# Which experts of the first sparse tile are added on TensorE: every third of the first 72 instead of the last 43

## The chip, the cores and the metric

One Trainium2 chip, of which the program uses one core. The metric is the time of one execution on the device in microseconds, as a median over runs. The core's engines are TensorE (PE, with its weight loads shown apart as PEld), VectorE (DVE), ScalarE (ACT), GpSimd (POOL) and SyncE (SP); each runs its own instructions in the order in which they stand in its queue and waits for the others by semaphores. Matrix products are accumulated in eight PSUM banks of 128 x 512 float32.

## What is computed

One decoder layer in float32 on 512 tokens of width 1024: an RMSNorm and one input projection; sparse attention (8 heads; compressed, selected and window branches) beside a diagonal state-space group; an output projection; then a product-key expert layer, and a last RMSNorm. The experts are where the change lies:

```python
s1 = einsum('bchd,kd->bchk', q[..., :half], sub1)
s2 = einsum('bchd,kd->bchk', q[..., half:], sub2)
v1, i1 = top_k(s1, 16); v2, i2 = top_k(s2, 16)
cand = v1[..., :, None] + v2[..., None, :]
cidx = i1[..., :, None] * 128 + i2[..., None, :]
top, sel = top_k(cand, 16)            # 16 of 16384 experts, for each of 8 heads
eidx = take_along_axis(cidx, sel); gate = softmax(top)
u_sel = u_tab[eidx]; v_sel = v_tab[eidx]
hid = einsum('bcd,bchkd->bchk', xb, u_sel)
act = gelu(hid) * gate
out = einsum('bchk,bchkd->bcd', act, v_sel)
```

So every token has 128 experts: a dot with a row of u, a gelu with a gate, and a row of v, times that number, added to the token.

## The kernel before

The tokens are four tiles of 128. Tiles 0 and 1 are sparse: for each k from 0 to 127 one indirect DMA, issued by POOL, gathers the k-th expert's u and v rows of all 128 tokens (128 x 2048 floats, 1.05 MB). Tiles 2 and 3 are dense: `dense` (l. 1215 to 1348) goes over all 16384 experts with matmuls, and its loop takes most of the second half of the program. Tile 1's experts all run inside that loop (class `Steps`, l. 1129), its adds on DVE.

Tile 0's experts run ahead of the loop, beside the generator `rest()` (l. 1461 to 1529): the projections of tiles 1 to 3 (keys, compressed keys and values, queries), `compress`, the attention of tile 1, the gated linear unit, the mix and the route of tile 1, beside it the attention and mix of tiles 2 and 3, and the route of tiles 2 and 3. A route ends in many small sorting steps on DVE (top 16 of 128, twice, then of the candidates). Each step of `rest()` yields a credit (table `W`, l. 1458), and the loop at l. 1544 to 1549 runs as many experts as the credit allows.

Expert k in the generator `peer` (l. 1070 to 1127): the gather is issued `ahead` = 2 experts early into a slot of a ring of five; DVE makes the dot into `hid` (l. 1098); ACT makes `act` in five steps (l. 1103 to 1107); and `lag` = 2 experts later the v row is added, in one of two ways that the lambda `HOW` (l. 1537) chooses:

- "V": DVE adds v times act to the token's row h (l. 1120).
- "P": ACT writes a diagonal matrix `dg` of act (l. 1115, three buffers), and PE adds dg times v to two PSUM banks `acc`, in two halves of 512 columns (l. 1117). The banks are taken at the first such expert (l. 1113) and held until `flush` (l. 1078) adds them to h after expert 127.

Behind the add the slot goes back to the ring (l. 1121), and the gather of expert k + 5 may use it. Ahead of the dense loop, all engines' orders are made by the framework's scheduler from program order, dependencies and its own timing of them (l. 1647); once written, each engine's queue is fixed. In the dense loop the order is pinned by hand. Every instruction passes the helper `issue`, so that all of them carry line 134; tiles tell them apart. `in_uv,eidx` is a gather, `junk` a dot, `zT` the projections' input, `more` scratch of keys, sorting and others.

Of the kernel before, what the change touches and what calls it, by code (L numbers as in the profile page):

```python
# [163 lines left out]
def hymba_kernel(ctx: ExitStack, tc: tile.TileContext, a, out, dbg=None):  # L164
    nc = tc.nc
    pins = set()
    V, S, G, PE = (Ordered(tc, e, n, pins) for e, n in ((nc.vector, "V"), (nc.scalar, "S"), (nc.gpsimd, "G"), (nc.tensor, "PE")))
# [902 lines left out]
    def peer(T, ring, ctl):  # L1070
# [20 lines left out]
        for k in range(128):  # L1091
# [15 lines left out]
            S.activation(act, g[:, 0:1], AF.Identity, scale=g[:, 2:3], bias=g[:, 2:3])  # L1107
            todo.append((t, uv[:, D:], act, HOW(T, k)))
            while len(todo) > ctl.lag or todo and k == 127:
# [423 lines left out]
        state["n0"] = True  # L1533
        yield from peer(1, uvr, ctl)

    KP = 85
    HOW = lambda T, k: "P" if T or k >= KP else "V"
    state = {}
    ctl = types.SimpleNamespace(ahead=2, lag=2, early=True)
    uvr = collections.deque(uvb + extra)  # L1540
# [110 lines left out]
```

## Time and profile before

| | us |
|---|---|
| runs before | 1639.01, 1633.65, 1630.3; median 1633.65 |
| profiled execution | 1637.53 |
| its span, all engines | 1635.8 |
| DVE busy | 1453.2 (89%) |
| PE busy | 1408.2 (86%) |
| ACT busy | 846.3 (52%) |
| POOL busy | 537.4 (33%) |
| granted TensorE clock, mean | 0.914 |
| first dot of tile 0 | at 227.4 |
| last dot of tile 0 | at 800.5 |
| dense loop in its even pace | from 876.9 |

The profile is one execution, with times in us from the start of its span; 1.7 us of the execution lie outside the span. Busy shares are means over stages that differ, so that a stage is read from its own window. The chain that ended last is 44% DVE and 33% PE. A granted clock of 1.00 is 2.4 GHz; a mean between a half and one in a window is a mixture of the two levels, 1.2 and 2.4 GHz.

### The profile page before, as it was taken

To read this page: it belongs to the slowest core of one execution; us is meant where nothing else is said; L and a number is where in the kernel's file an instruction comes from. 1 tells how busy PE (TensorE), PEld (TensorE's weight loads), DVE (VectorE), ACT (ScalarE), POOL (GpSimd) and SP (SyncE) were. 2 spreads that over 40 slices of the span, in tenths; PEclk is the share of its full clock that TensorE was granted. 3 is DMA by queue.
4 is the path that set the end of the run, shared out by engine and by line. 5 is a ranking of instruction groups with operands and counts; after the bars stand their busy time and mean duration, and the time that the engine had idled before them with its cause. 6 is when DMAs were issued, how large, how long until landed. Compare 5 with 4: busy or idle time off the path is not lost.

```text
span 1635.8 us, 24303 instructions
## 1 busy us (share of the span) xinstructions
PE 1408.2 (86%) x8348; PEld 1096.7 (67%) x8348; DVE 1453.2 (89%) x3369; ACT 846.3 (52%) x2069; POOL 537.4 (33%) x383
## 2 busy tenths in 40 slices
PE   5687794689866799997668999999999999999996
PEld 2366482455344456762357888888888999999995
DVE  8986279968999846899798999999999999999998
ACT  1335433644455652355565555555555555555553
POOL 6522012745344100233201333333343333333331
PEclk9897897787866799999958999999999999999998
DMA  6231478878998725488815999999999999999994
GB/s 260 104 104 65 167 295 299 338 293 318 358 341 305 283 102 208 155 320 325 322 61 198 337 335 337 339 340 343 339 333 357 394 372 381 374 373 382 374 375 173
DMA packets 88967, 469.47 MB, mean 287 GB/s; under 512 B 10252, under 2 KB 10892, under 8 KB 50700
## 3 DMA queue, kind: packets, MB, share of 16 engines
q0 software_dynamic: 37152, 268.98, 42.5%
q1 hardware_dynamic: 51692, 198.94, 33.8%
q8 instruction: 65, 1.06, 0.2%
q14 instruction: 58, 0.48, 0.1%
HBM read 464.74 MB, written 3.15 MB: 286 GB/s over the span
## 4 chain that ended last, share of the span: by engine, by line
DVE 44%; PE 33%; issue 12%; DMA 5%; ACT 3%; POOL 2%; SPq 0%; DVEq 0%; POOLq 0%; ACTq 0%
PE bank L134 33%; DVE X L134 25%; DVE lo L134 8%; DVE junk L134 7%; DMA X<-in_uv,eidx 4%; ACT X L134 2%; POOL X L134 2%; DVE act L134 1%; DMA raw<-in_uvt 1%; DMA X<-in_wq 1%; DVE nm L134 1%; DVE more L134 1%; DMA X<-in_x 0%; ACT gt L134 0%; DVE zT L134 0%
## 5 line engine op out<-in xcount | busy, mean ns | idle before, releaser
L134 POOL DMA_INDIRECT X<-in_uv,eidx x256 | 445.9, 1742 | 935.2 <-DVE X L134 689.4
L134 ACT ACTIVATE X<-bank 128x256 f32<-128x256 f32 (+4 forms) x423 | 213.9, 519 | 193.6 <-PE bank L134 147.0
L134 PE MATMUL bank<-hi,act 128*128 128x512 f32 x1024 | 299.7, 394 | 0.0
L134 PE MATMUL bank<-XH,hi 128*128 128x256 f32 x1024 | 288.2, 281 | 4.9 <-ACT hi L134 4.9
L134 PE MATMUL bank<-X 128*128 128x64 f16 (+10 forms) x1768 | 238.9, 283 | 60.4 <-DVE X L134 38.4
L134 PE MATMUL bank<-XH,lo 128*128 128x256 f32 x1024 | 287.2, 280 | 0.0
L134 PE MATMUL bank<-XL,hi 128*128 128x256 f32 x1024 | 286.9, 280 | 0.0
L134 DVE CUSTOM_DVE_ANT_0 junk<-X 128x1024 bf16<-128x1024 f32 x206 | 251.2, 1220 | 9.1 <-DMA X<-in_uv,eidx 5.4
L134 DVE TENSOR_TENSOR X<-X 128x256 f32<-128x256 f32 (+13 forms) x611 | 231.0, 411 | 25.3 <-ACT X L134 20.1
L134 ACT ACTIVATE gt<-hid 128x1 f32<-128x1 f32 x384 | 63.8, 198 | 358.8 <-DVE hid L134 358.5
L134 DVE SCALAR_TENSOR_TENSOR X<-X,act 128x1024 f32<-128x1024 f32 x179 | 229.0, 1279 | 4.6 <-ACT act L134 4.6
L134 DVE TENSOR_TENSOR lo<-raw,hi 128x1024 fp32r<-128x1024 f32 x172 | 209.9, 1220 | 3.6 <-ACT hi L134 3.6
L134 PEld LDWEIGHTS bank<-hi,act 128*128 128x128 f32 x1024 | 183.3, 188 | 32.7
L134 PEld LDWEIGHTS bank<-XH,hi 128*128 128x128 f32 x1024 | 193.4, 189 | 9.9 <-ACT hi L134 5.0
L134 PEld LDWEIGHTS bank<-XL,hi 128*128 128x128 f32 x1024 | 192.7, 188 | 4.9
L134 PE MATMUL bank<-X,X 128*128 128x128 f32 (+7 forms) x888 | 178.7, 375 | 19.4 <-ACT X L134 11.1
L134 PEld LDWEIGHTS bank<-XH,lo 128*128 128x128 f32 x1024 | 193.6, 189 | 0.0
L134 ACT ACTIVATE hi<-raw 128x1024 fp32r<-128x1024 f32 x172 | 179.0, 1053 | 26.6 <-PE bank L134 21.7
L134 PEld LDWEIGHTS bank<-X,X 128*128 128x128 f32 (+4 forms) x888 | 121.7, 197 | 63.8 <-issue 29.6
L134 PE MATMUL bank<-lo,act 128*128 128x512 f32 x512 | 159.5, 393 | 0.4 <-DVE lo L134 0.4
L134 PEld LDWEIGHTS bank<-X 128*128 128x128 f32 (+3 forms) x744 | 117.8, 197 | 61.1 <-issue 37.4
L134 PEld LDWEIGHTS bank<-lo,act 128*128 128x128 f32 x512 | 95.9, 188 | 22.7 <-DVE lo L134 0.8
(202 smaller groups left out, 1802.3 us busy)
## 6 DMA issues: line engine op xcount, KB each, us to landing
raw<-in_uvt SPq DMA_DIRECT2D x172, 512.0 KB, 7.6
X<-in_uvt SPq DMA_DIRECT2D x84, 512.0 KB, 7.9
X<-in_wq SPq DMA_DIRECT2D x24, 1024.0 KB, 4.5
X<-in_wo SPq DMA_DIRECT2D x8, 1024.0 KB
X<-in_x SPq DMA_DIRECT2D x8, 512.0 KB, 9.0
X<-in_wB SPq DMA_DIRECT2D x4, 1024.0 KB, 15.7
X<-in_wA SPq DMA_DIRECT2D x4, 1024.0 KB, 7.6
X<-in_w SPq DMA_DIRECT2D x4, 1024.0 KB
```

The source lines that it names most:

```text
L134: ins = self.last = f(*args, **kw)
```

## The change

`HOW` is another rule. Before, tile 0's experts 85 to 127 (43 of them) took "P". Now experts 2, 5, 8, ..., 71 (24 of them) do, and 104 take "V". The two banks are thus taken at expert 2, and released as before behind expert 127. Tile 1 inside the dense loop is the same. No other line is changed, but the scheduler's order of all that stands ahead of the loop is another.

```diff
--- before.py
+++ after.py
@@ -1533,8 +1533,8 @@
         state["n0"] = True
         yield from peer(1, uvr, ctl)
 
-    KP = 85
-    HOW = lambda T, k: "P" if T or k >= KP else "V"
+    KP = 72
+    HOW = lambda T, k: "P" if T or k < KP and k % 3 == 2 else "V"
     state = {}
     ctl = types.SimpleNamespace(ahead=2, lag=2, early=True)
     uvr = collections.deque(uvb + extra)
```

PE's queue at the first diagonal product (dg). Ahead of it stand now, in the kernel after, the projections of tiles 1 to 3:

```order
L134 MATMUL bank0_83<-X_76,zT0_111 128x512 x4
L134 MATMUL bank0_83<-X_76,zT1_112 128x512 x4
L134 MATMUL bank4_87<-X_76,zT0_111 128x512 x3
L134 MATMUL bank4_87<-X_76,zT1_112 128x512 x4
L134 MATMUL bank2_85<-X_76,dg_1939 128x512
L134 MATMUL bank1_84<-X_76,dg_1939 128x512
L134 MATMUL bank6_89<-X_76,zT0_111 128x512 x3
L134 MATMUL bank7_90<-c_ident_105,X4_77 128x128 x4
L134 MATMUL bank6_89<-X_76,zT0_111 128x512
L134 MATMUL bank6_89<-X_76,zT1_112 128x512 x4
```

and stood, in the kernel before, the mix of tiles 2 and 3 (bank3 with x32) and the route of tile 1 (c_subT); bank3 is then the first accumulator:

```order
L134 MATMUL bank7_90<-c_ident_105,X5_78 128x128 x4
L134 MATMUL bank4_87<-c_ident_105,X5_78 128x128 x4
L134 MATMUL bank3_86<-X4_77,X_76 128x128 x32
L134 MATMUL bank1_84<-c_subT_132,X4_77 128x128 x4
L134 MATMUL bank3_86<-X_76,dg_4369 128x512
L134 MATMUL bank3_86<-X_76,dg_4400 128x512
```

The first product has moved from expert 85 to expert 2, some 370 rows up in the queue.

POOL's queue behind the first ten gathers of tile 0 (DMA ... in_uv). After, five in one row, four, and one are followed by the rotation of tile 1's keys (c_rope), and the next gather waits for PE:

```order
L134 DMA X<-in_uv,eidx_1302 128x2048 x5
L134 DMA X_77<-in_uv,eidx_1302 128x2048 x4
L134 DMA X<-in_uv,eidx_1302 128x2048
L134 TENSOR_TENSOR X_77<-more,c_rope 128x64
L134 TENSOR_TENSOR X_77<-more,c_rope 128x4x8 x2
L134 TENSOR_TENSOR more<-X_77 128x4x16
L134 TENSOR_TENSOR more<-X_77,c_rope 128x64
```

Before, seven more gathers stood between those ten and the same rotation, and others among its steps:

```order
L134 DMA X<-in_uv,eidx_1302 128x2048 x6
L134 DMA X_77<-in_uv,eidx_1302 128x2048 x4
L134 DMA X<-in_uv,eidx_1302 128x2048 x3
L134 DMA X_77<-in_uv,eidx_1302 128x2048 x2
L134 DMA X<-in_uv,eidx_1302 128x2048 x2
L134 TENSOR_TENSOR X_77<-more,c_rope 128x64
L134 TENSOR_TENSOR X_77<-more,c_rope 128x4x8 x2
L134 DMA X<-in_uv,eidx_1302 128x2048
L134 TENSOR_TENSOR more<-X_77 128x4x16
L134 DMA X_77<-in_uv,eidx_1302 128x2048
```

The gathers moved behind the rotations of tiles 1 to 3.

DVE's queue at the last dot of tile 0 (ISA junk). After, it stands among the sorting steps (MAX, MAX_INDEX) of the routes of tiles 2 and 3:

```order
L134 MAX more<-bank_88 128x8
L134 ISA junk,hid<-X 128x1024
L134 ISA hid 128x1
L134 SCALAR_TENSOR_TENSOR X<-X,act 128x1024
L134 TENSOR_TENSOR X_77<-X_77 128x2x64
L134 MAX_INDEX X_78<-more,X_77 128x8
L134 MAX more<-X_78 128x8
```

Before, the sums of the two accumulators and the preparation of the dense loop followed on it:

```order
L134 ISA junk,hid<-X 128x1024
L134 ISA hid 128x1
L134 TENSOR_TENSOR X<-bank_86,X 128x512
L134 TENSOR_TENSOR X<-bank_84,X 128x512
L134 TENSOR_TENSOR X<-X 128x512
L134 TENSOR_TENSOR X<-X 128x1024
```

The sorting steps that stood ahead of the last dots now stand behind: 409 instructions are between the last dot of tile 0 and the first of tile 1, where 143 were.

## Rows read from the trace of the kernel before

**Rows 1.** Windows of the core, one row for each stretch: from and to in us, then its length; busy us and instructions of PE, PEld, DVE, ACT and POOL; the mean granted TensorE clock as a share of full speed; the busy share of the DMA engines; GB/s.

```profile
227.40:318.80 91.40, 51.10 (x222) 33.55 (x221) 85.40 (x284) 38.60 (x146) 41.32 (x34) 0.78 0.85 320
318.80:363.40 44.60, 40.64 (x178) 25.69 (x176) 31.21 (x49) 23.27 (x72) 22.13 (x22) 0.89 0.83 327
363.40:562.20 198.80, 147.35 (x575) 82.77 (x575) 185.07 (x390) 100.95 (x392) 83.48 (x55) 0.73 0.87 329
562.20:672.20 110.00, 107.35 (x533) 72.45 (x534) 62.74 (x316) 43.66 (x107) 1.55 (x2) 0.95 0.34 123
672.20:800.40 128.20, 110.48 (x369) 62.16 (x367) 124.77 (x566) 76.81 (x290) 45.25 (x39) 0.99 0.84 312
800.40:876.90 76.50, 51.71 (x603) 41.77 (x604) 64.97 (x153) 46.19 (x56) 4.36 (x4) 0.67 0.32 118
876.90:1250.00 373.10, 361.98 (x2644) 325.64 (x2644) 371.06 (x542) 209.90 (x390) 134.43 (x61) 1.00 0.93 338
```

**Rows 2.** Timeline of DVE at four places: the first dot of tile 0 (CUSTOM_DVE_ANT_0 into junk), the last row of expert indices with the dots and adds behind it, and the first dot after the long pause of the gathers. Columns: start, us, engine, line, operation, out<-in, count, and in brackets the idle time before it and what released it.

```profile
227.37 1.23 DVE L134 CUSTOM_DVE_ANT_0 junk<-X 128x1024 bf16<-128x1024 f32 x1 [0.59 <-DMA X<-in_uv,eidx]
...
318.79 0.18 DVE L134 SCALAR_TENSOR_TENSOR eidx<-X 128x32 int32<-128x32 f32 x1
318.89 1.22 DVE L134 CUSTOM_DVE_ANT_0 junk<-X 128x1024 bf16<-128x1024 f32 x1
...
320.03 1.28 DVE L134 SCALAR_TENSOR_TENSOR X<-X,act 128x1024 f32<-128x1024 f32 x1
321.23 1.22 DVE L134 CUSTOM_DVE_ANT_0 junk<-X,X 128x1024 bf16<-128x1024 f32 x1
...
678.40 1.22 DVE L134 CUSTOM_DVE_ANT_0 junk<-X 128x1024 bf16<-128x1024 f32 x1
```

**Rows 3.** Groups of DVE instructions by operation and shape between 227.4 and 800.5 us: busy us, mean ns of one, idle time before them and its releasers. CUSTOM_DVE_ANT_0 are the dots, SCALAR_TENSOR_TENSOR with act the adds, each in two spellings of the tiles' names; MAX8 is a sorting step.

```profile
L134 DVE CUSTOM_DVE_ANT_0 junk<-X 128x1024 bf16<-128x1024 f32 x78 | 95.0, 1218 | 8.0 <-DMA X<-in_uv,eidx 5.4 <-issue 1.4 <-ACT act L134 1.2
L134 DVE SCALAR_TENSOR_TENSOR X<-X,act 128x1024 f32<-128x1024 f32 x51 | 65.2, 1279 | 4.6 <-ACT act L134 4.6
L134 DVE CUSTOM_DVE_ANT_0 junk<-X,X 128x1024 bf16<-128x1024 f32 x50 | 61.5, 1229 | 4.7 <-DMA X<-in_uv,eidx 4.7
L134 DVE SCALAR_TENSOR_TENSOR X<-X,act,X 128x1024 f32<-128x1024 f32 x34 | 43.4, 1277 | 6.1 <-ACT act L134 5.9
L134 DVE MAX8 X<-X 128x8 f32<-128x112 f32 x56 | 13.0, 266 | 0.0
```

**Rows 4.** Waits between 562.2 and 672.2 us: engine and tile that waited, for whom; us in total, times, the longest.

```profile
POOL X L134 <- DVE more L134: 75.7, 1, 75.7
DVE X L134 <- PE bank L134: 36.6, 7, 14.5
POOL X L134 <- PE bank L134: 34.3, 1, 34.3
```

**Rows 5.** Timeline of POOL from 555 us, columns as in rows 2. DMA_INDIRECT is the issue of one expert's gather.

```profile
559.74 0.96 POOL L134 DMA_INDIRECT X<-in_uv,eidx  x1 [3.68 <-DVE X L134]
594.99 1.53 POOL L134 IOTA X<- 128x256 f16 x1 [34.29 <-PE bank L134]
672.17 0.96 POOL L134 DMA_INDIRECT X<-in_uv,eidx  x1 [75.66 <-DVE more L134]
```

**Rows 6.** Timeline of PE from 604 us. X,X 128x128 x58 are mixing matmuls, c_subT and 128x256 those of the routes, dg the diagonal products (two passes for each half of a v row).

```profile
608.37 21.98 PE L134 MATMUL bank<-X,X 128*128 128x128 f32 x58
...
640.95 2.74 PE L134 MATMUL bank<-X,dg 128*128 128x512 f32 x6
...
670.88 1.02 PE L134 MATMUL bank<-X,dg 128*128 128x512 f32 x2
...
675.19 1.88 PE L134 MATMUL bank<-X,dg 128*128 128x512 f32 x4
676.91 1.03 PE L134 MATMUL bank<-X 128*128 128x256 f32 x4
```

**Rows 7.** All instructions on the tile dg: duration in ns (least, median, greatest), first and last start, shapes.

```profile
L134 PE MATMUL bank<-X,dg x172: 592/592/1057, 641.0 to 804.8; 128*128 128x512 f32 x172
L134 ACT ACTIVATE dg<-c_ident,act x43: 385/402/415, 559.4 to 802.9; 128x128 f32<-128x128 f32 x43
```

**Rows 8.** Timeline of PE at the projections of tiles 1 to 3 (zT) and their key transposes (c_ident,more).

```profile
297.48 1.11 PE L134 MATMUL bank<-c_ident,more 128*128 128x128 f32 x4 [34.98 <-ACT more L134]
299.28 5.68 PE L134 MATMUL bank<-X,zT 128*128 128x280 f32 x16 [0.69 <-ACT X L134]
...
308.96 5.73 PE L134 MATMUL bank<-X,zT 128*128 128x280 f32 x16 [3.02 <-ACT X L134]
...
338.08 2.74 PE L134 MATMUL bank<-X,zT 128*128 128x512 f32 x6
```

**Rows 9.** Timeline of POOL in the same time: gathers, and the first rotation of keys (c_rope).

```profile
268.36 1.69 POOL L134 DMA_INDIRECT X<-in_uv,eidx  x1 [5.64 <-DVE X L134]
...
290.21 1.69 POOL L134 DMA_INDIRECT X<-in_uv,eidx  x1 [1.11 <-DVE X L134]
292.23 2.36 POOL L134 TENSOR_TENSOR X<-more,c_rope 128x64 f32<-128x64 f32 x3 [0.33 <-ACT more L134]
```

## The prediction

> **What bounds the kernel now.** I read the busy time of the engines in stretches first [rows 1], since the shares over the whole span mix stages. From 876.9 us on the dense loop keeps VectorE (DVE) busy 371.06 of 373.10 us and TensorE (PE) 361.98, at a granted clock of 1.00. The loop ends where its own work ends, and the change leaves that work alone, so every microsecond won or lost before 876.9 is one of the whole kernel. The stretch to look at runs from the first dot of tile 0 at 227.37 [rows 2] to 876.9: 649.5 us, in which DVE's busy times (85.40, 31.21, 185.07, 62.74, 124.77, 64.97) add up to 554.2 and its idle time to 95.3. DVE is the bound of all but one of its windows: idle are 6.0, 13.4, 13.7, then 47.3 in 562.2 to 672.2, and 3.4 and 11.5 [rows 1].
>
> Most of DVE's work there is tile 0's: 128 dots of about 1.22 us and 85 adds of 1.28 us [rows 3].
>
> The one weak window is a knot, not a lack of work. In 562.2 to 672.2 the waits [rows 4] name GpSimd (POOL) first: one wait of 75.7 us, put down to a DVE instruction. In POOL's timeline the gathers stop after 559.74, an iota at 594.99 waits 34.29 us for PE, and the next gather starts at 672.17 [rows 5]. What holds the ring is the first TensorE adds: PE comes to the first diagonal product (dg) only at 640.95, since the products stand in its queue behind 21.98 us of mixing matmuls and the route of tile 1, whose banks they take over [rows 6]. The first expert's second half runs at 670.88 and the next gather 1.3 us later [rows 5, 6]. Meanwhile the transfers run at 0.34 of the DMA engines' time, against 0.87 in the window before [rows 1].
>
> **What the change does.** Before, experts 85 to 127 were added on PE, 43 of them; now 2, 5, ..., 71, which are 24. Three things follow.
>
> **DVE gets 19 adds more.** 19 x 1.279 = 24.3 us [rows 3]. ScalarE (ACT) loses 19 diagonals of 0.40 us [rows 7], PE 19 x 4 passes. Four passes take 1.72 us, from 675.19 to 676.91 [rows 6], so PE loses 33 us, but in windows in which DVE, not PE, has the least idle time (672.2 to 800.4: 124.77 of 128.20) [rows 1]. I cost that at nothing: DVE's work covers it, and were the cover gone it would be a gain of up to 33. The DVE work to 876.9 becomes 554.2 + 24.3 = 578.5. The end of the stretch is then 227.4 + 578.5 + idle, and the question of the whole change is DVE's idle time. Under 71.0 us (95.3 - 24.3) the kernel gains, above it loses.
>
> **The knot of 562 to 672 goes.** From expert 72 to the end no add needs PE, so the ring runs through the mix of tiles 2 and 3 and the routes of tiles 2 and 3. In the new order the first mix add of tile 2 stands behind dot 79, before behind dot 90, and dots 88 to 128 stand between the sorting steps of the last routes. The work that waited at 562 to 672 for PE has dots and adds to fill it. In turn the last dot comes earlier in DVE's queue: 409 DVE instructions instead of 143 stand between it and tile 1's first dot, by estimate some 118 us of work: the 64.97 us of 800.4 to 876.9 [rows 1] and 266 instructions more at about 0.2 us, as most are sorting steps (a MAX8 takes 0.27 [rows 3]). That is work moved, not added. So the 47.3 us are free to fall to the rate of the other windows.
>
> **A new wait comes in front.** The first diagonal product is now that of expert 2, and PE's queue has it behind almost all projections of tiles 1 to 3. Gather 7 needs expert 2's slot, and POOL's queue now has all gathers from there on behind it. So ten gathers are issued, and then none until PE has come to that product. DVE stands with seven dots done where it had twenty-two done at the last index row (318.79). It reaches that row earlier by 15 dots at 1.14 and 16 adds at 1.20 (318.89 to 320.03 to 321.23) [rows 2]: 17.1 + 19.2 = 36.3, so at about 282. When is PE there? Before, PE waited 34.98 us until 297.48 for the rotated keys [rows 8], because POOL's rotations stood among gathers that each waited for DVE: the first rotation starts at 292.23, the gathers between run from 268.36 [rows 9]. Now the rotations stand right behind the ten gathers and can start near 272, 20 us sooner, so PE's 297.48 becomes 277.5. From there to the end of the projections (338.08 + 2.74 = 340.8) are 43.3 us [rows 8], of which about 7 now stand behind the product: 277.5 + 43.3 - 7 = 314 at most, some 312. The gather behind it lands 6.2 us later (issued 672.17, dot at 678.40) [rows 2, 5]: 318. DVE would be idle from 282 to 318, **36 us**. Lower bound 20, if part of the projections that waited for POOL close up (PE had gaps of 0.69 and 3.02 us between them) and what DVE has of compress work fills some; upper bound 45, if the rotations gain nothing over half of the 20 us. I take 36, as worked out. Before, the same windows to 363.4 held 6.0 + 13.4 us of idle time, of which I keep the 6.0.
>
> **Then the steady part.** From the eighth dot to the last DVE has 578.5 - 53 (up to the eighth dot: 85.40 - 36.3, and some 4 of compress work) - 118 (the tail) = 407 us of work. At the rate of 363.4 to 562.2, 13.7 idle for 185.07 busy [rows 1], that is **30 us** idle. At the rate of 672.2 to 800.4 (3.4 for 124.77) it would be 11. I take 30, because this part holds attention and the early half of the adds, as that window did. The transfers say the same: before, from 318.8 to 800.4, the windows moved 14.6 + 65.4 + 13.5 + 40.0 = 133.5 MB; now about fifteen more gathers of 1.05 MB fall behind 318, so 149 MB. At 329 GB/s they take 453 us, to 771, and DVE by its own sum comes to 318 + 407 + 30 = 755. Both are near, so DMA hardly lets DVE run denser than I assume.
>
> **The 24 products themselves.** In place of a DVE add, gather k+5 now waits for ACT's diagonal, then for PE's queue. The trace shows no such product in this stretch. From below they cost nothing, as the four passes of 675.19 did in their window. From above they cost what they take at half clock. In 363.4 to 562.2 PE's granted clock was 0.73 on average, so much of it ran at the lower level, 1.2 GHz; a pass took 592 ns at the least and 1057 at the most [rows 1, 7]. The doubled four passes are 3.4 us; 24 x 1.7 = 41 us more, if all came to DVE. I take **5 us**, nearer to nothing, because PE is idle 51 us in that window and an add comes two experts after its dot.
>
> The Trainium skill's page "TensorE: Matmul & The Clock Gate" (Part 1: The HAM clock gate) says that the throttled clock is the default and that steady activity lifts it. The row of 0.73 with PE busy 147 of 199 us agrees, and so does 0.99 in the window after; by that rule alone the products would be priced at 3.4 us each in a waiting PE, which is the second rival's sum below.
>
> **The tail.** 800.4 to 876.9 had 11.5 us idle [rows 1], partly waits for loads that now have sorting work beside them; I take **8**.
>
> **Sum.** Idle 6 + 36 + 30 + 5 + 8 = 85 us, against 95.3: 10 us of idle time are won and 24.3 us of work added. The net is +14 us. The profiled execution took 1637.53 us (span 1635.8), which gives 1651.5; the median of the three runs, 1633.65, gives 1647.7. I predict against the median, **1648 us**, 0.9% slower. About 0.5%, 8 us, is what a measurement of this kernel can tell from no change.
>
> **Rivals.** *Faster: the filled knot outweighs the adds.* If the hold in front is 20 us and the steady part lies midway between the two rates (20), with nothing for the products and 9 for the tail, idle is 55: 55 - 71 = -16, **1618 us**. For it: the knot is 47.3 us, nearly twice the added work, and the clock of 0.95 to 0.99 in the later windows shows PE with work in hand. Against it: the new hold costs most of what the knot gives back. It decides as soon as idle time falls below 71.
>
> [...]
>
> *Slower by more: PE becomes the pacer.* The 24 products stand in order between attention's matmuls, at the lower clock, and two PSUM banks are held from expert 2 to expert 127, so that the attention and the mixes have six banks instead of eight for all that time. A PE that waits for DVE's softmax steps then delays a gather, which delays the dots, which stand ahead of the next softmax step. Priced with three quarters of the 41 us, 30 more: idle 115, +44, **1678 us**. For it: PE's clock and the 36.6 us that DVE waited for PE's banks in the knot [rows 4]. Against: most of PE's time in the window is slack. It decides if a product waits over 1.5 us on average.
>
> *No change.* The hold is 25 and the rest as above, less the 5: idle 69, **1632 us**. That the change doesn't do what it says would show here too: if the ring held the gathers at 562 for another reason than the products, the knot stayed and the time went to +24 and beyond, but POOL's resumption 1.3 us after the second half speaks against that.
>
> **How the numbers follow.** Forecast (+8 to +30) 0.38; slower by more 0.14; within 8 us 0.25; faster 0.23. The range leaves out half of the fast case and half of the slowest: 1617 to 1677. Slower 0.52, same 0.25, faster 0.23. The first two cases hold half the chance, with their own range 1642 to 1677.
>
> **What would show it.** In the new trace: no pause of POOL's gathers over 20 us after 360 us; a pause of some 30 us in front with the eleventh gather released by PE near 312; DVE busy about 578 us from first dot to the start of the loop, idle about 85; the loop itself unchanged at 1.00 and begun near 891. Wrong would be: a short hold (PE reaches the first product before 300), or a steady part with DVE idle far from 30 us, or many small POOL waits for PE.

## The result: 1.2% slower

The changed kernel takes 1657.3 us (median of 1648.19, 1655.38, 1659.22 and 1661.0), against 1634.6 for the kernel before (1630.3 to 1639.01). The ratio is 1.0116 with a 95% interval of 1.0085 to 1.0148, about 19 us; the two medians lie 22.7 us apart. The profiled execution of the changed kernel is the fastest of its four, 1648.19 us (span 1646.4), 10.7 us over that of before.

These are the windows of the changed kernel, with the columns of [rows 1]. They are cut at the first dot of tile 0, at the end of its seventh dot and the start of its eighth, at the attention, at the mixes, at the last dot, and at the second dot of tile 1. The two rows at the end are the stretch as a whole and what follows it.

```profile
224.70:261.90 37.20, 32.47 (x152) 20.45 (x151) 34.42 (x165) 12.89 (x44) 5.55 (x6) 1.00 0.76 285
261.90:311.80 49.90, 37.44 (x125) 22.59 (x126) 17.31 (x80) 15.40 (x38) 9.52 (x23) 0.86 0.38 138
311.80:360.50 48.70, 44.00 (x173) 22.74 (x172) 37.46 (x82) 27.53 (x102) 19.29 (x17) 0.75 0.66 250
360.50:557.70 197.20, 176.67 (x749) 93.16 (x749) 170.83 (x400) 119.90 (x423) 75.67 (x56) 0.91 0.90 341
557.70:660.00 102.30, 81.83 (x396) 58.03 (x395) 94.28 (x293) 46.49 (x167) 30.66 (x24) 0.90 0.91 361
660.00:752.70 92.70, 30.50 (x121) 25.15 (x119) 92.70 (x250) 39.66 (x162) 30.89 (x28) 0.67 0.84 306
752.70:821.00 68.30, 18.97 (x86) 15.69 (x86) 66.31 (x374) 18.08 (x57) 1.89 (x2) 0.60 0.20 70
821.00:887.50 66.50, 49.94 (x588) 41.87 (x589) 59.49 (x135) 43.91 (x46) 1.70 (x1) 0.59 0.18 64
...
224.70:887.50 662.80, 471.82 (x2383) 299.68 (x2383) 572.81 (x1769) 323.86 (x1038) 175.18 (x154) 0.80 0.69 259
887.50:1646.40 758.90, 732.36 (x5031) 661.49 (x5029) 738.49 (x1057) 429.81 (x792) 261.71 (x125) 0.99 0.93 347
```

And the same two stretches of the kernel before:

```profile
227.40:876.90 649.50, 508.62 (x2476) 318.39 (x2475) 554.15 (x1751) 329.49 (x1059) 198.10 (x154) 0.83 0.70 264
876.90:1635.80 758.90, 731.80 (x5023) 660.68 (x5022) 738.43 (x1057) 429.64 (x792) 264.36 (x125) 0.99 0.93 347
```

The last row of each settles where not to look: 758.90 us behind the cut in both, with DVE busy 738.49 and 738.43. All of the difference lies in the stretch from the first dot of tile 0 on, 662.8 us against 649.5. There DVE works 18.7 us more (572.81 against 554.15) and is idle 90.0 us against 95.3. By windows the 90.0 are 2.8, then 32.6 between the seventh and the eighth dot (49.90 less 17.31), then 11.2, 26.4, 8.0 and 0.0 to the last dot, then 2.0 and 7.0. The 47.3 us of idle time that stood in one window [rows 1] are gone from there; 32.6 us now stand at the front.

Three timelines of the changed kernel show the front: DVE at the seventh dot, the last index row, the steps of `compress` (c_peT) and the eighth dot; POOL at the tenth gather, the first rotation, the eleventh gather, and the gather behind the longest later pause; PE at the first product.

```profile
260.72 1.23 DVE L134 CUSTOM_DVE_ANT_0 junk<-X 128x1024 bf16<-128x1024 f32 x1
...
276.34 0.19 DVE L134 SCALAR_TENSOR_TENSOR eidx<-X 128x32 int32<-128x32 f32 x1
290.58 1.92 DVE L134 TENSOR_TENSOR X<-X,c_peT 128x496 f32<-128x496 f32 x2 [14.05 <-PE bank L134]
...
310.79 1.00 DVE L134 TENSOR_TENSOR X<-X,c_peT 128x496 f32<-128x496 f32 x1 [18.19 <-PE bank L134]
311.83 1.23 DVE L134 CUSTOM_DVE_ANT_0 junk<-X 128x1024 bf16<-128x1024 f32 x1
```

```profile
265.81 0.95 POOL L134 DMA_INDIRECT X<-in_uv,eidx  x1 [3.04 <-DVE X L134]
272.81 0.76 POOL L134 TENSOR_TENSOR X<-more,c_rope 128x64 f32<-128x64 f32 x3 [6.06 <-DVE X L134]
...
306.30 0.98 POOL L134 DMA_INDIRECT X<-in_uv,eidx  x1 [0.27 <-PE bank L134]
...
751.72 0.95 POOL L134 DMA_INDIRECT X<-in_uv,eidx  x1 [8.65 <-DVE more L134]
```

```profile
304.14 1.88 PE L134 MATMUL bank<-X,dg 128*128 128x512 f32 x4
```

The rotation starts at 272.81 where it started at 292.23 [rows 9]; the first product runs at 304.14; the next gather goes out at 306.30 and its dot starts at 311.83. DVE has reached the last index row at 276.34. Next in its queue are steps of `compress`, which need projections from PE, and it waits 14.05 and 18.19 us for them. The last of these steps starts at 310.79, just as the gather of 306.30 is about to land, so the wait for `compress` and the wait for the gather end within about a microsecond of each other. From there on the ring runs: between 360 us and the last gather, POOL's longest wait in front of one is 8.65 us, where it was 75.66 [rows 5].

### The profile page after: what moved, and what is told of

It is laid out like the page before. It is cut to its first block, busy times and chain, and to the rows that moved or that the text cites. A ratio compares the mean times of both kernels' runs of the same rounds, so it can differ in the third digit from the quotient of the medians.

```text
span 1646.4 us, 24108 instructions
## 1 busy us (share of the span) xinstructions
PE 1370.8 (83%) x8272; PEld 1077.3 (65%) x8272; DVE 1473.1 (89%) x3388; ACT 840.6 (51%) x2048; POOL 511.2 (31%) x383
## 4 chain that ended last, share of the span: by engine, by line
DVE 44%; PE 36%; issue 11%; DMA 4%; ACT 3%; POOL 1%; SPq 0%; DVEq 0%; POOLq 0%; ACTq 0%
PE bank L134 36%; DVE X L134 26%; DVE lo L134 8%; DVE junk L134 6%; DMA X<-in_uv,eidx 3%; ACT X L134 2%; DVE act L134 1%; POOL X L134 1%; DVE more L134 1%; DVE nm L134 1%; DMA X<-in_x 0%; DVE hid L134 0%; ACT gt L134 0%; DVE zT L134 0%; DVE f_r L134 0%
## 5 line engine op out<-in xcount | busy, mean ns | idle before, releaser
L134 POOL DMA_INDIRECT X<-in_uv,eidx x256 | 427.7, 1671 | 969.3 <-DVE X L134 807.6
L134 PE MATMUL bank<-X 128*128 128x64 f16 (+10 forms) x1768 | 231.8, 279 | 110.7 <-DVE X L134 93.7
L134 ACT ACTIVATE X<-bank 128x256 f32<-128x256 f32 (+7 forms) x423 | 214.6, 520 | 208.8 <-PE bank L134 154.1
L134 DVE TENSOR_TENSOR X<-X 128x256 f32<-128x256 f32 (+14 forms) x611 | 230.7, 413 | 23.9 <-ACT X L134 19.2
L134 DVE SCALAR_TENSOR_TENSOR X<-X,act 128x1024 f32<-128x1024 f32 x191 | 244.5, 1280 | 6.3 <-ACT act L134 6.2
L134 PEld LDWEIGHTS bank<-hi,act 128*128 128x128 f32 x1024 | 183.3, 188 | 32.7
L134 ACT ACTIVATE hi<-raw 128x1024 fp32r<-128x1024 f32 x172 | 179.1, 1054 | 22.8 <-PE bank L134 21.7
L134 PE MATMUL bank<-X,X 128*128 128x128 f32 (+7 forms) x888 | 172.1, 363 | 17.7 <-ACT X L134 13.8
L134 PEld LDWEIGHTS bank<-X,X 128*128 128x128 f32 (+4 forms) x888 | 115.2, 187 | 64.8 <-issue 27.3
L134 PE MATMUL bank<-c_ident,X 128*128 128x128 f32 (+2 forms) x300 | 49.0, 304 | 79.9 <-DVE X L134 46.4
```

The source lines that it names most:

```text
L134: ins = self.last = f(*args, **kw)
```

## Experiments

Each experiment changes the line of `HOW`, and where said a few more. The stretch is from tile 0's first dot to tile 1's second dot in the profiled run, with DVE's busy time in it and the rest of it as idle time. A ratio is to runs of the kernel before that were taken beside that kernel: their median was 1634.6 for the changed kernel, 1634.5 for the runs e1 to e4, 1636.9 for those with b and 1636.7 for those with f and l. A difference of two medians from different groups is therefore good to about 2 us; where it matters, the difference by the ratios stands beside it.

| kernel | products | median us | ratio to before (95%) | stretch | DVE busy | DVE idle |
|---|---|---|---|---|---|---|
| before | 85..127 | 1634.6 | 1 | 649.4 | 554.1 | 95.3 |
| changed | 2, 5, .., 71 | 1657.3 | 1.0116 (1.0085 to 1.0148) | 662.8 | 572.8 | 90.0 |
| e1_from20 | 20, 23, .., 71 | 1671.6 | 1.0241 (1.0198 to 1.0283) | 686.8 | 582.6 | 104.2 |
| e2_none | none | 1633.5 | 0.9997 (0.9974 to 1.0019) | 643.0 | 598.1 | 44.9 |
| e3_split | 20, .., 71 and 96..127 | 1635.3 | 0.9990 (0.9966 to 1.0013) | 647.0 | 545.2 | 101.8 |
| e4_last28 | 100..127 | 1618.4 | 0.9897 (0.9860 to 0.9934) | 632.0 | 570.0 | 62.0 |
| b_after | as changed, banks early | 1662.0 | 1.0144 (1.0121 to 1.0168) | 671.0 | 574.4 | 96.6 |
| b_before | as before, banks early | 1650.3 | 1.0077 (1.0061 to 1.0094) | 663.8 | 556.6 | 107.2 |
| b_third | 2, 5, .., 125, banks early | 1657.0 | 1.0115 (1.0094 to 1.0137) | 671.2 | 556.0 | 115.1 |
| b_none | none, banks early | 1656.6 | 1.0124 (1.0107 to 1.0141) | 667.4 | 600.4 | 67.0 |
| f_one2 | 2 alone | 1657.0 | 1.0131 (1.0094 to 1.0169) | 668.8 | 599.8 | 69.1 |
| f_after | as changed, banks back at 71 | 1655.9 | 1.0129 (1.0095 to 1.0162) | 670.9 | 573.4 | 97.5 |
| l_104 | 104..127 | 1621.0 | 0.9909 (0.9872 to 0.9946) | 633.6 | 573.6 | 60.0 |
| l_108 | 108..127 | 1621.4 | 0.9914 (0.9879 to 0.9948) | 635.3 | 576.4 | 58.9 |

**No hold in front: products from 20 on.**

```diff
-    HOW = lambda T, k: "P" if T or k < KP and k % 3 == 2 else "V"
+    HOW = lambda T, k: "P" if T or 20 <= k < KP and k % 3 == 2 else "V"
```

> Diagonal products for every third expert from 20 to 71 (18 of them), so none before the projections of tiles 1 to 3 are through. Theory A (the loss sits in the hold in front, 32.6 us of DVE idle time between the seventh and the eighth dot, and in the 19 adds): the hold falls to about 10 us as in the kernel before, and six adds more cost 7.7 us, so 15 us less than the changed kernel: about 1642 us. Rival B (the loss sits in the products themselves, which stand in order between attention's matmuls): the six products in front hardly matter, 1657 plus some 5, 1662 us.

1671.6 us: neither theory A nor rival B. The hold did not go, it moved along with the first product and grew. ACT makes the diagonal at 320.03, and PE runs the product's two halves at 387.94 and 397.68. DVE works 32.29 of the 84.8 us from 322.2 on (timelines of ACT and PE, and the window):

```profile
320.03 0.40 ACT L134 ACTIVATE dg<-c_ident,act 128x128 f32<-128x128 f32 x1
```

```profile
387.94 1.02 PE L134 MATMUL bank<-X,dg 128*128 128x512 f32 x2
...
397.68 1.02 PE L134 MATMUL bank<-X,dg 128*128 128x512 f32 x2
```

```profile
322.20:407.00 84.80, 83.93 (x340) 46.38 (x339) 32.29 (x95) 23.84 (x65) 6.16 (x10) 0.88 0.37 133
```

PE was busy all through, 83.93 of 84.80 us, with `compress` and attention, and the two halves, ready together, run ten us apart. That looks like two banks that came free one after the other, which this run does not show; the runs with the banks taken early, below, try the idea on other kernels. What this run refutes is that a first product behind the projections has no hold.

**No product at all, and one alone.**

```diff
+    HOW = lambda T, k: "P" if T or False else "V"     # e2_none
```

> No diagonal product for tile 0: all 128 adds on DVE, 43 more than before (55 us) and 24 more than in the changed kernel (30.7 us). Theory A (idle time of DVE is the knot before and the hold after): neither knot nor hold, DVE idle about 50 us of the stretch up to the dense loop, so 1634 + 55 - 45 = 1644 us. Rival B (products pace attention): idle falls below 30, so under 1625 us. Rival C (idle time is what it is, each add on DVE costs its 1.28 us): 1634 + 55 = 1689 us.

1633.5 us, no change against the kernel before, though DVE has 44 us more of work: idle time fell to 44.9, where theory A had 50 and rival B under 30. Theory A's time is 10 us too long; it priced the 43 adds at 55 us, and DVE's busy time grew by 44. Rival C is out by 55 us.

```diff
+    HOW = lambda T, k: "P" if T or k == 2 else "V"
+    LASTP = 2
...
                 ring.append(t)
+                if T == 0 and j == LASTP:     # j: the expert just added
+                    flush()
```

> One product alone, expert 2, with its two banks given back right behind it; the other 127 adds on DVE. It has the hold of the changed kernel in front, and neither its other 23 products nor two banks held. Theory A (the hold costs what DVE idles in it): the 1633.5 of all adds on DVE and some 28 us, about 1660 us. Rival H (DVE's lead is lost in front but regained later; the loss is made by the other products and the held banks): about 1636 us.

1657.0 us, on theory A's side. PE runs the product, the next gather goes out behind it, and the eighth dot, released by that gather, starts at 312.93 (timelines of PE, POOL and DVE of f_one2):

```profile
305.06 1.88 PE L134 MATMUL bank<-X,dg 128*128 128x512 f32 x4
...
307.22 0.98 POOL L134 DMA_INDIRECT X<-in_uv,eidx  x1 [0.27 <-PE bank L134]
...
312.93 1.27 DVE L134 CUSTOM_DVE_ANT_0 junk<-X 128x1024 bf16<-128x1024 f32 x1 [0.20 <-DMA X<-in_uv,eidx]
```

The next rows are windows: between the seventh and the eighth dot, from the eighth to the last, and the whole stretch, first with expert 2 on PE (f_one2), then with no product (e2_none):

```profile
264.47:312.93 48.46, 38.11 (x126) 23.02 (x127) 20.70 (x79) 15.39 (x38) 11.14 (x23) 0.86 0.27 91
312.93:759.44 446.51, 310.93 (x1373) 198.49 (x1371) 417.28 (x1018) 225.10 (x832) 160.56 (x124) 0.77 0.87 331
228.64:897.47 668.83, 443.50 (x2305) 294.41 (x2304) 599.77 (x1792) 315.53 (x1017) 179.50 (x154) 0.74 0.68 257
```

```profile
270.90:272.91 2.01, 0.00 (x0) 0.00 (x0) 2.01 (x7) 1.41 (x6) 0.83 (x1) 0.50 0.37 82
272.91:722.72 449.81, 338.43 (x1473) 218.06 (x1474) 417.12 (x1003) 236.99 (x857) 184.04 (x143) 0.80 0.86 331
228.62:871.57 642.95, 436.79 (x2304) 293.68 (x2304) 598.08 (x1791) 315.53 (x1018) 196.89 (x154) 0.76 0.70 267
```

The first row of each tells it: with the product 48.46 us lie between the two dots and DVE works 20.70 of them, without it 2.01, all worked. Idle time is 27.8 us more there, 3.5 less behind (29.2 against 32.7), and 24.2 more over the stretch (69.1 against 44.9). One product of four passes costs 23.5 us of the median (1657.0 - 1633.5; 22 by the ratios), as much as the change costs in all. The other 23 products, with the two banks held for them, thus bring the changed kernel nothing: behind the eighth dot they take 22 us from DVE's work (395 in the sum of its windows, against 417) and give 16 of them back as idle time (45.6 against 29.2) in the profiled runs, and the medians differ by 0.3 us. No run separates the products from the banks held up to expert 71. In the traces the added idle time does not stand in waits for PE's banks (13.0 us in the changed kernel, 15.4 in f_one2) but in waits for gathers (12.9 against 5.5) and for ACT (17.7 against 7.1), which speaks for the products.

**The other end: the last 28, 24 and 20.**

```diff
+    HOW = lambda T, k: "P" if T or k >= 100 else "V"     # or 104, 108
```

> The last 28 experts, 100 to 127, on TensorE instead of the last 43. Theory A (the knot is the first product's place behind the mix and the route of tile 1; moved behind these it is gone): 15 adds more cost 19 us, some 37 us of idle time go, about 1617 us. Rival D (the knot moves along with the first product): 1634 + 19, about 1653 us.

> The last 24 experts, 104 to 127, on TensorE: as many products as in the changed kernel, all of them behind the route of tile 1. If the number of adds sets the time, it is the changed kernel's 1657 us. If the place of the products sets it (no hold in front, the wait for the first product beside sorting steps), it is that of the last 28 and four adds, about 1622 us.

> The last 20 experts, 108 to 127, on TensorE. Four adds more than with 24: 4 us slower than those if DVE's work is the price, about 1626 us; faster, some 1615 us, if the wait for the first product shrinks by more than that.

1618.4, 1621.0 and 1621.4 us. With the last 24 there are as many products and as many DVE adds as in the changed kernel, and the time is 36 us less (34 by the ratios): the place of the products decides, not their number. Theory A had the time of the last 28 to 2 us, but not by its mechanism. The knot did not go, it moved with the first product, as rival D said; the gathers of that kernel still pause for 82.95 us (POOL's timeline, then the window of that pause between two dots and the one behind it, to the last dot):

```profile
610.95 1.68 POOL L134 DMA_INDIRECT X<-in_uv,eidx  x1 [4.79 <-DVE X L134]
695.58 0.94 POOL L134 DMA_INDIRECT X<-in_uv,eidx  x1 [82.95 <-DVE X L134]
```

```profile
617.00:703.50 86.50, 85.56 (x410) 65.97 (x410) 68.18 (x393) 25.42 (x74) 2.84 (x3) 1.00 0.35 131
703.50:781.30 77.80, 60.20 (x162) 29.06 (x160) 77.22 (x351) 43.26 (x171) 26.00 (x21) 0.96 0.76 283
```

In that pause DVE now works 68.18 of 86.50 us, because the sorting steps of the routes of tiles 2 and 3 stand there, where it worked 62.74 of 110.00 in the kernel before [rows 1]. A pause of the ring costs what DVE idles in it, 18.3 us here; the pause of 82.8 us between two dots with the last 24 costs 12.2, that of 72.4 with the last 20 costs 16.1. Behind it PE takes the products in a window in which DVE has no time to spare (77.22 of 77.80) and PE has.

**Both ends.**

```diff
+    HOW = lambda T, k: "P" if T or (20 <= k < KP and k % 3 == 2 or k >= 96) else "V"
```

> Every third expert from 20 to 71, and all from 96 to 127, on TensorE (50 products). Theory A (DVE is the bound after the knot, PE has room in the last third): 32 adds less than with the first group alone, 41 us, so about 1602 us. Rival D (a product late in PE's queue holds the ring wherever it stands behind the mix and the routes, so a knot forms at 96 as it did at 85): 40 us of DVE idle time come back, about 1640 us.

1635.3 us, near rival D's figure, but not by its mechanism. The loss is the hold at expert 20, as in the first experiment (81.3 us between dots 25 and 26, 51.3 of them idle); in the second group POOL's longest wait in front of a gather is 9.2 us. Set against 1671.6, the 32 products at the end save 36 us of the 41 expected. Here the banks had already been taken, and the products late in the queue held nothing up.

**The two banks taken early.**

```diff
+    HELD = {0: [bank(), bank()]}     # ahead of rest()
...
                     if not acc:
-                        acc.extend([bank(), bank()])
+                        acc.extend(HELD.pop(T, None) or [bank(), bank()])
```

> The changed kernel, with one thing more: the two accumulator banks are taken before the projections of tiles 1 to 3 are written, not at expert 2, so that they have no earlier user that runs late. Theory E (the first product waits for the earlier user of the two banks that it gets from the rotation): the hold of 32.6 us falls to some 5, 28 us less than the changed kernel, about 1629 us. Rival F (the product stands late in PE's queue for other reasons): the hold stays, about 1657 us.

> The kernel before (experts 85 to 127 on TensorE), with the two banks taken ahead of the projections. Theory E: the first product no longer waits for banks of the route, the knot of 47 us goes, DVE's work is the same, about 1590 us. Rival F (PE's queue is full of mixing and route matmuls, and the products stand behind them): about 1634 us. Rival G (six banks in place of eight slow the attention and the mix): above 1640 us.

> Every third expert of all 128 on TensorE (42 products), the two banks taken ahead of the projections. Theory E: DVE work as in the kernel before, no hold and no knot, idle time some 55 us, about 1595 us. Rival B (products between attention's matmuls pace the ring): about 1640 us or more.

> No product for tile 0, but two banks taken ahead of the projections and given back behind expert 127, unused: the price of six banks by itself. Theory E: with no hold there is nothing to win, and six banks are enough: about 1633 us, as with all adds on DVE and eight banks. Rival G: PE and DVE wait for each other's banks, some 20 us more, about 1653 us.

Theory E had the place right and the time wrong, by 33, 60, 62 and 24 us (the last kernel gives its banks back behind expert 127). With the banks in hand the first product of the changed kernel runs at 250.29 instead of 304.14, and the eighth dot at 270.35 instead of 311.83; the first product of the kernel before runs at 550.5 instead of 641.0 [rows 7]. So the banks handed to the first product set its place. But other waits came. In b_after the dots pause 27.4 us from 334.2 on, 20.1 of them idle. These are the rows of PE at the first product, then of POOL, PE and ACT at that pause:

```profile
250.29 1.88 PE L134 MATMUL bank<-X,dg 128*128 128x512 f32 x4
```

```profile
355.94 0.98 POOL L134 DMA_INDIRECT X<-in_uv,eidx  x1 [9.55 <-PE bank L134]
```

```profile
324.69 19.05 PE L134 MATMUL bank<-X,zT 128*128 128x512 f32 x44
343.57 1.02 PE L134 MATMUL bank<-X,dg 128*128 128x512 f32 x2
...
354.59 2.79 PE L134 MATMUL bank<-X,dg 128*128 128x512 f32 x6
```

```profile
334.23 0.40 ACT L134 ACTIVATE dg<-c_ident,act 128x128 f32<-128x128 f32 x1
```

ACT makes the diagonal of that product at 334.23. PE is then in a run of projections that lasts until the product's first half at 343.57, and `compress` stands between that and the second half, so the gather goes out at 355.94. That is rival B's mechanism, in a place where theory E had nothing. In b_third POOL waited 31 times for such products, 94.2 us in all. And b_none, without a single product, shows what taking two banks went with: 1656.6 against 1633.5, 23 us (21 by the ratios), where rival G had 20. Its last dot comes 13 us earlier than with eight banks (709.91 against 722.72), and then DVE idles 21.7 of 185.39 us, against 8.8 behind the last dot of e2_none:

```profile
709.91:895.30 185.39, 122.09 (x938) 104.52 (x939) 163.66 (x737) 73.38 (x134) 2.84 (x2) 0.71 0.14 49
227.94:895.30 667.36, 449.52 (x2296) 298.14 (x2295) 600.38 (x1791) 317.07 (x1016) 193.44 (x154) 0.75 0.67 257
```

But its order differs in more than banks: the window behind the last dot has 737 DVE instructions, where that of e2_none has 599. So the 23 us are those of two banks and of the order that the scheduler then made, and no run separates the two. Rival G's threshold for b_before, above 1640, held as well (1650.3).

**The banks given back at 71.** The same `flush` as for one product, with LASTP = 71.

> The changed kernel with its two banks added to the tokens and given back behind expert 71 instead of 127, so that the second half of tile 0 has eight banks. Rival G (six banks slow the mix and the routes, as two unused held banks cost 23 us): 10 to 20 us less than the changed kernel, 1640 to 1647 us. Theory A (hold and products make the loss): no change, about 1657 us.

1655.9 us, no change: the banks held behind expert 71 are not what makes the changed kernel slow. From expert 72 on six banks were as good as eight. What the two cost up to expert 71 this run does not show.

## Why the prediction was right

1648 us was forecast, 1647.7 - 1633.65 = 14 us slower; 1657.3 was measured, a ratio of 1.0116 or 19 us, within the range of 1617 to 1677 and within that of the first two cases. The mechanism was the forecast one: the knot went, a hold came in front, and DVE's idle time did not fall by enough to pay for the added adds. That the stretch of the profiled pair grew by 13.3 us against the 14 forecast is in part luck, as DVE's work grew 5.6 us less than forecast and its idle time came out 5 us longer. Two of the three signs of being wrong did show: the steady part idled 45.6 us instead of about 30, and POOL waited for PE's products many times. By steps:

- **The frame held.** The loop behind the cut is unchanged to 0.1 us.
- **The added adds** were mis-sized: 18.7 us of DVE's busy time, not 24.3. The durations of the adds themselves rose as priced: by shape they sum to 109.9 us in the stretch before and to 134.6 after, 24.7 more, at the same mean of 1.28 us. But the busy time counts once what overlaps, and an add overlaps its neighbour (1.20 us from start to start [rows 2] would give 22.8). The rest lies in other instructions of DVE, small steps above all, which overlap by some 4 us more than before. The other runs, too, come to about 1 us of busy time for one add: 43 more in e2_none are 44.0, 15 more in e4_last28 are 15.9.
- **The hold in front** was right in each link: rotations at 272.81 for "near 272", the first product at 304.1 for 312, the gather's dot at 311.83 for 318, DVE at its last index row at 276.3 for 282, idle 32.6 us for 36. One link was not in it: what DVE waits for in the trace is PE's projections, for its steps of `compress`, and that wait ends together with the gather's. f_one2 shows that the hold alone costs as much as the whole change. What was left out is why the product stands behind the projections: b_after shows that the banks it is handed put it there.
- **The knot went**, as said, and 8.0 us idle remain in 557.7 to 660 and none in 660 to 752.7. The cause was named, but as one of that place in the queue: a first product behind mixes and a route. In e1_from20 and e4_last28 the wait travels with the first product, wherever that is. With products starting at 2 it is the hold itself.
- **The steady part** was too low: 45.6 us idle (11.2 + 26.4 + 8.0 + 0.0) for 30 + 5. The figure without products, 32.7 in e2_none and 29.2 in f_one2, agrees with the 30. So the term that was too small is the price of the products, 5 us, where about 13 to 16 were paid, if the two held banks cost nothing up to expert 71.
- **That products would cost half clock** was the upper bound; it did not come. In the window of before with 0.73 [rows 1] the changed kernel shows the first of these rows; the second is f_one2 with one product, the third f_after with 24:

```profile
363.40:562.20 198.80, 178.66 (x765) 94.81 (x765) 172.45 (x410) 122.80 (x433) 75.58 (x56) 0.91 0.91 343
363.40:562.20 198.80, 146.99 (x592) 83.14 (x588) 180.29 (x367) 102.63 (x381) 75.60 (x54) 0.74 0.85 322
363.40:562.20 198.80, 173.59 (x716) 88.50 (x715) 166.20 (x384) 115.99 (x413) 71.33 (x54) 0.91 0.89 331
```

PE is busy 178.66 us instead of 147.35, and the granted clock is 0.91 instead of 0.73. A pass took 593 ns in the median. POOL waited for these tiles 20 times, 43.2 us in all, which is 1.8 us for each of the 24 products. That is over the 1.5 us by which the rival of a pacing PE was to be decided, and the steady part did come out longer, but by 11 us and not by that rival's 30. The rows are all instructions of PE on the tile dg in the changed kernel, then who waited for it:

```profile
L134 PE MATMUL bank<-X,dg x96: 592/593/1223, 304.1 to 549.3; 128*128 128x512 f32 x96
...
  POOL X L134: 43.2, 20
```

The Trainium skill's page "TensorE: Matmul & The Clock Gate" (Part 1: The HAM clock gate) has activity lift the clock. The runs agree: this window has 0.72 to 0.75 in the seven kernels with no product in it (before, e2_none, e4_last28, b_none, f_one2, l_104, l_108), and 0.86 to 0.91 in the six with products spread over it (changed, e1_from20, e3_split, b_after, b_third, f_after). I had drawn the opposite price from the page, by taking the clock of before as given. Two readings beside it were loose: the 0.99 is that of the second window after, the next one has 0.95 [rows 1], and the second rival's sum takes three quarters of the 1.7 us that half clock adds to a product, not 3.4 us for each.

- **The tail** idled 9.0 us for 8, and the first window 2.8 for 6.
- **Of the 19 us only 10.7 show in the profiled pair**: 13.3 of the stretch less a first dot that came 2.7 us earlier. The profiled run was the fastest of the changed kernel, so the windows above show less than the median pays. f_after, whose order in front of expert 71 is near the same, has 33.5 us in the hold and 52.7 instead of 45.6 behind it, at a span of 1654.4. That points to the steady part as the place where the executions differ, but it is not shown; what makes it vary stays open.

## What to carry to other kernels

In this kernel an accumulator taken from a rotating pool of banks waited for whoever had used them last in program order (the first product ran 54 us sooner with its banks taken early), and everything that waits for its first product, here a ring of gathers in one queue, waited too. The first product alone cost 22 to 24 us against none at all, and 24 products at the right place gained 12 to 14. Before moving work to an engine with room, look at what will wait for its first instruction, and whether the busy engine has other work to do in that pause. A pause of 82 to 86 us between two dots cost 12 to 18 us of idle time where sorting steps stood, and 52 where they did not. Of the kernels here the one with the last 28 experts on TensorE has the least time, 0.9897 of that before; the last 24 and the last 20 are not clearly apart from it (0.9909 and 0.9914).

## What the runs showed that was not expected

DVE doing all 128 adds is as fast as with 43 of them on PE (0.9997, with 0.9974 to 1.0019): 44 us of work went into idle time that was there. The granted clock rose from 0.73 to 0.91 in a window in which PE got 31 us more of busy time. And two PSUM banks that nobody uses, held from ahead of the projections on, went with 21 to 23 us (the order of the queues differed too), while two held from expert 72 on in the changed kernel went with none.
